# Attention softmax in an encoder kernel: sum with the bias and maximum in one operation by quarters, probabilities normalised on ScalarE

## The chip, the core and the metric

The kernel runs on one core of a Trainium2 chip. The core's engines run beside each other, each with a queue of its own that is worked off in order: TensorE (PE; its weight loads are listed as PEld), VectorE (DVE), ScalarE (ACT), GpSimd (POOL) and SyncE (SP, which issues DMAs). They meet through semaphores. The metric is the device time of one execution in microseconds; lower is better.

## The reference

An encoder of 2 layers over x of 512 positions by 1024 channels in float32. A layer is

```
x += 1/2 * SwiGLU(RMSNorm(x))
x += W_o( g_na * NA(h) W_na + g_f * FNet(h) W_f ),   h = RMSNorm(x)
x += 1/2 * SwiGLU(RMSNorm(x))
```

and a final RMSNorm ends it. NA is neighbourhood attention on the grid of 8 rows by 64 columns, with 8 heads of 64 channels. The columns go in 4 blocks of 16 queries; a block sees a band of 32 key columns, so a query has 8 x 32 = 256 keys, of which those outside its window of 16 columns are masked:

```
s = einsum(q, k) * 64 ** -0.5 + bias        # bias: learned, relative, per head
s = where(col_ok, s, -inf)
p = softmax(s, axis=-1)                     # over 256 keys
o = einsum(p, v)
```

FNet is the real part of a 2-D Fourier transform per channel group. The change is inside the softmax.

## The kernel before

All matmuls are made in float32 precision from two rounded parts: a helper `split` (L286 to L292) has ACT write the rounded high part and DVE the difference, and `mm3` (L281 to L284) issues three matmuls, high by high, high by low, low by high. Weights come by DMA in granules of 128 x 1024 (L150, on SP; some are added to another by a DMA of POOL at L152) and are split in this way two granules ahead of their use; L288 and L289 are the two lines of it, and L291 and L292 the same with a scale. The SwiGLU stages and the gates use Strassen's products.

`stage_mixer` goes, per layer: norm, projections for the Fourier part and for v, the Fourier part, then attention, then the gates (in an order written out by hand for DVE and ACT) and the output.

Attention works on two heads at a time (`hp` of 0 to 3) and on two of the four query blocks at a time (`pr`), so it has 8 steps. One step i of the pipeline `att_step` issues three things: `att_out(i-2)` (probabilities by v, and the split of the result `o`), `att_trans(i-1)` (transposes of the probabilities on PE at L1003, two PSUM banks, each split into `p` by L288 and L289) and `att_scores(i)`. Behind each of steps 0 to 4 stands a projection of a next q or k (24 matmuls; `proj_T` multiplies by the norm's row R at L826 and splits); between the later ones stand rows of the Fourier output product (`fill`, whose results ACT copies out at L1058).

`att_scores` computes for both heads e the scores of 128 queries against 256 keys, for two blocks jj side by side: one PSUM bank of 128 x 512 per head, L972. A quarter below is one head and one block, 128 x 256. Then, before the change:

- DVE adds the bias tile (bias and mask together) to each bank and writes the 128 x 512 tile `s` in SBUF (L980), and takes the negated maximum of each quarter (L981, one instruction per head).
- ACT takes the exponential of each quarter with the negated maximum as its per-partition bias and sums it on the way (L987).
- DVE takes the reciprocal of the two sums of a head (L990) and multiplies the head's two quarters by them (L992).

The bias tiles `bm` are built by POOL (L955), which waits until DVE's L980 of two head pairs earlier has read the tile that it overwrites.

The program is written in one order. A planner then lays the instructions out on the engines before the run: by their place in the program, by when its own costs say that their inputs are due, and by free tiles; it fixes each engine's order. Only inside `tc.manual_schedule` does an engine keep the written order; attention is not inside one.

Of the kernel before, what the change touches and what calls it, by code (L numbers as in the profile page):

```python
# [13 lines left out]
AF = mybir.ActivationFunctionType  # L14
ALU = mybir.AluOpType
AX = mybir.AxisListType

P = 128
# [10 lines left out]
NEG = -1.0e30  # L29
# [63 lines left out]
def encoder_kernel(  # L93
# [3 lines left out]
    V, S, G, PE = nc.vector, nc.scalar, nc.gpsimd, nc.tensor  # L97
# [11 lines left out]
    def nm(s):  # L109
        uid[0] += 1  # L110
        return f"{s}_{uid[0]}"
# [8 lines left out]
    def bank(s="ps"):  # L120
        return pp.tile([P, T], F32, tag="ps", name=nm(s))
# [663 lines left out]
    def stage_mixer(l, norm, nxt):  # L785
        mp = mix_pool[0]

        def tmp(dt=F32, s="x"):
            return mp.tile([P, T], dt, tag="tmp", name=nm(s), bufs=8)
# [142 lines left out]
        o, q, k, bms = [], {}, {}, {}  # L932
# [28 lines left out]
        def att_scores(i):  # L961
            hp, pr = divmod(i, 2)
            (qh, ql), (kh, kl) = q[hp], k[hp]
            ps = [bank(), bank()]
            for jj in range(2):
                j = 2 * pr + jj
                ks = slice(BAND[j] * 64, BAND[j] * 64 + 256)
                qs = slice(j * P, (j + 1) * P)
                for i, (a, b) in enumerate(((qh, kh), (qh, kl), (ql, kh))):
                    for e in range(2):  # L970
                        r = slice(64 * e, 64 * e + 64)
                        PE.matmul(  # L972
                            ps[e][:, jj * 256 : (jj + 1) * 256], a[r, qs], b[r, ks], start=i == 0, stop=i == 2
                        )
            s_ = [tmp(s="s"), tmp(s="s")]
            nmx = sp.tile([P, 4], F32, tag="nmx", name=nm("nmx"), bufs=4)
            sm = sp.tile([P, 4], F32, tag="sm", name=nm("sm"), bufs=4)
            rs = sp.tile([P, 4], F32, tag="rs", name=nm("rs"), bufs=4)
            for e in range(2):
                V.tensor_tensor(s_[e], ps[e], bms[hp][e][:, pr : pr + 2, :].rearrange("p a b -> p (a b)"), ALU.add)  # L980
                V.tensor_reduce(  # L981
                    nmx[:, 2 * e : 2 * e + 2], s_[e].rearrange("p (a k) -> p a k", a=2), AX.X, ALU.max, negate=True
                )
            for e in range(2):
                for jj in range(2):
                    c, z = slice(jj * 256, (jj + 1) * 256), 2 * e + jj
                    S.activation(  # L987
                        s_[e][:, c], s_[e][:, c], AF.Exp, bias=nmx[:, z : z + 1], accum_out=sm[:, z : z + 1]
                    )
                V.reciprocal(rs[:, 2 * e : 2 * e + 2], sm[:, 2 * e : 2 * e + 2])  # L990
                se = s_[e].rearrange("p (a k) -> p a k", a=2)
                V.tensor_tensor(  # L992
                    se, se, rs[:, 2 * e : 2 * e + 2].unsqueeze(2).to_broadcast([P, 2, 256]), ALU.mult
                )
            return s_

        def att_trans(s_):
# [32 lines left out]
        def att_step(i):  # L1030
            if 0 <= i - 2 < 8:
                att_out(i - 2, pt_.pop(i - 2))
            if 0 <= i - 1 < 8:
                pt_[i - 1] = att_trans(sc.pop(i - 1))
            if i < 8:
                sc[i] = att_scores(i)
# [152 lines left out]
        bias = []  # L1189
# [281 lines left out]
```

## Time and profile before

| what | value |
|---|---|
| time, median of 3 runs | 1946.33 us (1942.85 to 1946.69) |
| time of the profiled execution | 1946.85 us |
| its span, first to last instruction | 1944.4 us |
| mean granted TensorE clock | 0.997 |
| attention of layer 1, of layer 2 | about 411 to 489 us, 1372 to 1450 us |
| exponentials, L987 | 64 of 128 x 256, mean 498 ns |

A row of a group reads: line, engine, operation, written tile <- read tiles, shapes, count, then busy time in us and mean ns of one, then the idle time of the engine just before them and what ended it. A row of a timeline reads: start in us from the span's start, length in us, engine, line, operation, tiles, count; the bracket is idle time before it and what ended that. The chain of waits is followed back from the last instruction: at each piece to what released it or to the instruction before it on its engine; a piece called issue is time in which the engine waited for nothing that the profile shows. The rows of the windows give a stretch and its length, then the busy time of each engine and its instructions, the clock, the DMA share and GB/s. All lines are of the code printed above.

### The profile page before, as it was taken

What the parts mean: (1) busy time and instruction counts of PE and PEld (TensorE: products, weight loads), DVE (VectorE), ACT (ScalarE), POOL (GpSimd) and SP (SyncE); (2) the same over time, 40 slices, a digit from 0 to 9 for tenths busy, and PEclk for the clock granted to TensorE, in tenths of its full rate; (3) what the DMA queues carried; (4) which work ended last, traced back from release to release, by engine and by line L of the source; (5) the groups of instructions that cost most, each with busy time, mean ns of one, the idle gap of its engine ahead of it and who ended that gap; (6) DMA issues with size and microseconds to landing.
All of it is one profiled execution on the core that took longest, in us unless ns stands there. A gap on an engine that the chain in (4) does not pass through costs nothing.

```text
span 1944.4 us, 24590 instructions
## 1 busy us (share of the span) xinstructions
PE 1912.6 (98%) x8997; PEld 1583.5 (81%) x8997; DVE 1624.1 (84%) x1945; ACT 1127.3 (58%) x1605; POOL 213.1 (11%) x252
## 2 busy tenths in 40 slices
PE   9999999999999999999999999999999999999996
PEld 7788888888778888888888888888887888888885
DVE  8878899698788877889977878996878887877998
ACT  6655666455556655566655556663555566555654
POOL 0001010300111010001000000102101110100012
PEclk9999999999999999999999999999999999999998
DMA  8777498321997567749857665965039975766692
GB/s 284 199 201 194 148 255 306 105 60 56 261 231 190 139 187 204 181 153 263 240 142 207 177 169 176 289 219 147 28 116 243 235 198 132 196 181 162 186 286 97
DMA packets 105448, 361.82 MB, mean 186 GB/s; under 512 B 12016, under 2 KB 14192, under 8 KB 105328
## 3 DMA queue, kind: packets, MB, share of 16 engines
q1 hardware_dynamic: 76848, 264.01, 39.7%
q0 software_dynamic: 27328, 94.39, 26.3%
q10 hardware_dynamic: 1152, 1.86, 0.3%
q8 instruction: 70, 1.15, 0.2%
q14 instruction: 50, 0.41, 0.1%
HBM read 354.97 MB, written 2.10 MB: 184 GB/s over the span
## 4 chain that ended last, share of the span: by engine, by line
PE 78%; DVE 13%; DMA 3%; issue 3%; ACT 3%; ACTq 0%; SPq 0%; POOL 0%; DVEq 0%; POOLq 0%
PE A L282 8%; PE A L284 8%; PE A L283 8%; PE o L283 5%; PE o L284 5%; PE o L282 5%; PE B L283 4%; PE B L284 4%; PE B L282 4%; PE ps L282 4%; PE ps L283 4%; PE ps L284 4%; DVE wlo L289 4%; DMA raw<-in_wst_dram 3%; PE C L283 2%
## 5 line engine op out<-in xcount | busy, mean ns | idle before, releaser
L289 DVE TENSOR_TENSOR wlo<-raw,whi 128x1024 fp32r<-128x1024 f32 (+1 forms) x522 | 628.1, 1209 | 252.9 <-ACT whi L288 251.9
L288 ACT ACTIVATE whi<-raw 128x1024 fp32r<-128x1024 f32 (+1 forms) x522 | 540.1, 1037 | 496.6 <-PE A L284 126.3
L152 POOL DMA_DIRECT2D raw<-in_wst_dram x152 | 131.2, 878 | 1338.4 <-DMA raw<-in_wst_dram 814.4
L170 DVE TENSOR_TENSOR raw<-raw,raw 128x1024 f32<-128x1024 f32 (+1 forms) x128 | 150.9, 1189 | 2.4
L283 PE MATMUL A<-wlo,xh 128*128 128x512 f32 x384 | 150.0, 391 | 2.8 <-DVE wlo L173 2.2
L284 PE MATMUL A<-whi,xl 128*128 128x512 f32 x384 | 149.6, 389 | 0.0
L282 PE MATMUL A<-whi,xh 128*128 128x512 f32 x384 | 149.4, 390 | 0.0
L172 ACT ACTIVATE whi<-raw 128x1024 fp32r<-128x1024 f32 x76 | 78.9, 1038 | 68.3 <-PE B L284 33.2
L173 DVE SCALAR_TENSOR_TENSOR wlo<-raw,whi 128x1024 fp32r<-128x1024 f32 x76 | 89.8, 1193 | 13.4 <-ACT whi L172 13.4
L283 PEld LDWEIGHTS A<-wlo,xh 128*128 128x128 f32 x384 | 72.1, 188 | 19.8 <-DVE wlo L173 4.0
L282 PEld LDWEIGHTS A<-whi,xh 128*128 128x128 f32 x384 | 71.9, 188 | 15.7 <-ACT whi L172 0.8
L284 PEld LDWEIGHTS A<-whi,xl 128*128 128x128 f32 x384 | 72.1, 188 | 14.9
L466 ACT ACTIVATE sn<-A 128x512 f32<-128x512 f32 x96 | 56.8, 598 | 41.8 <-PE A L284 41.7
L282 PE MATMUL A<-whi,t3h 128*128 128x512 f32 x192 | 75.1, 391 | 2.4 <-ACT sn L466 2.4
L282 PE MATMUL B<-whi,t1h 128*128 128x512 f32 x192 | 76.1, 398 | 0.4 <-ACT whi L288 0.4
L283 PE MATMUL A<-wlo,t2h 128*128 128x512 f32 x192 | 74.8, 390 | 0.5 <-DVE wlo L289 0.5
L283 PE MATMUL C<-wlo,xh 128*128 128x512 f32 x192 | 74.8, 390 | 0.5 <-DVE wlo L289 0.5
L283 PE MATMUL B<-wlo,t1h 128*128 128x512 f32 x192 | 75.0, 391 | 0.2
L282 PE MATMUL C<-whi,xh 128*128 128x512 f32 x192 | 74.8, 391 | 0.2 <-ACT whi L288 0.2
L282 PE MATMUL A<-whi,t2h 128*128 128x512 f32 x192 | 74.9, 392 | 0.0
L283 PE MATMUL A<-wlo,t3h 128*128 128x512 f32 x192 | 74.9, 390 | 0.0
L284 PE MATMUL B<-whi,t1l 128*128 128x512 f32 x192 | 74.9, 390 | 0.0
(352 smaller groups left out, 4944.1 us busy)
## 6 DMA issues: line engine op xcount, KB each, us to landing
raw<-in_wst_dram SPq DMA_DIRECT2D x463, 512.0 KB
raw<-in_wst_dram POOLq DMA_DIRECT2D x168, 512.0 KB, 7.8
raw<-in_wst_dram SPq DMA_DIRECT2D x30, 256.0 KB
vs<-v SPq DMA_DIRECT2D x12, 256.0 KB
bw<-in_rpb_dram SPq DMA_DIRECT2D x32, 68.0 KB
x<-in_xin_dram SPq DMA_DIRECT2D x4, 512.0 KB
raw<-in_wst_dram POOLq DMA_DIRECT2D x8, 256.0 KB, 8.4
dft<-in_dft_dram POOLq DMA_DIRECT2D x8, 256.0 KB, 5.4
```

The costliest lines, as they stand in the source:

```text
L152: G.dma_start(out=self.t, in_=wst[GRAN_AT[self.plus]][:, 0 : self.n], accum_op=ALU.add)
L170: V.tensor_tensor(t, t, self.add.t, ALU.add)
L172: S.activation(hi, t, AF.Copy, scale=-1.0)
L173: V.scalar_tensor_tensor(lo, t, -1.0, hi.bitcast(F32), ALU.mult, ALU.subtract)
L282: PE.matmul(ps, lh, rh, start=start, stop=False, skip_group_check=again)
L283: PE.matmul(ps, lh, rl, start=False, stop=False, skip_group_check=again)
L284: PE.matmul(ps, ll, rh, start=False, stop=stop, skip_group_check=again)
L288: S.activation(hi, src, AF.Copy)
L289: V.tensor_tensor(lo, src, hi.bitcast(F32), ALU.subtract)
L466: S.activation(t[:, b, :], ps[b], AF.Copy)
```

## The change

The sum with the bias is made by quarters, with an operation that also gives the quarter's minimum: it writes s = -(scores + bias) and, beside it, the minimum of s, started from 1e30. That minimum is the negated maximum of the sum. The exponentials undo the sign with a scale of -1. After the exponentials and reciprocals of both heads, ACT multiplies each quarter by its reciprocal as a copy with a per-partition scale; DVE's multiplication goes. So one step has on DVE 4 such sums and 2 reciprocals in place of 2 sums, 2 maxima, 2 reciprocals and 2 products, and on ACT 4 exponentials and 4 copies in place of 4 exponentials.

```diff
             for e in range(2):
-                V.tensor_tensor(s_[e], ps[e], bms[hp][e][:, pr : pr + 2, :].rearrange("p a b -> p (a b)"), ALU.add)
-                V.tensor_reduce(
-                    nmx[:, 2 * e : 2 * e + 2], s_[e].rearrange("p (a k) -> p a k", a=2), AX.X, ALU.max, negate=True
-                )
+                for jj in range(2):
+                    c, z = slice(jj * 256, (jj + 1) * 256), 2 * e + jj
+                    V.tensor_tensor_reduce(
+                        s_[e][:, c], ps[e][:, c], bms[hp][e][:, pr + jj, :], -1.0, -NEG, ALU.add, ALU.min, nmx[:, z : z + 1]
+                    )
             for e in range(2):
                 for jj in range(2):
                     c, z = slice(jj * 256, (jj + 1) * 256), 2 * e + jj
                     S.activation(
-                        s_[e][:, c], s_[e][:, c], AF.Exp, bias=nmx[:, z : z + 1], accum_out=sm[:, z : z + 1]
+                        s_[e][:, c], s_[e][:, c], AF.Exp, scale=-1.0, bias=nmx[:, z : z + 1], accum_out=sm[:, z : z + 1]
                     )
                 V.reciprocal(rs[:, 2 * e : 2 * e + 2], sm[:, 2 * e : 2 * e + 2])
-                se = s_[e].rearrange("p (a k) -> p a k", a=2)
-                V.tensor_tensor(
-                    se, se, rs[:, 2 * e : 2 * e + 2].unsqueeze(2).to_broadcast([P, 2, 256]), ALU.mult
-                )
+            for e in range(2):
+                for jj in range(2):
+                    c, z = slice(jj * 256, (jj + 1) * 256), 2 * e + jj
+                    S.activation(s_[e][:, c], s_[e][:, c], AF.Copy, scale=rs[:, z : z + 1])
             return s_
```

## The prediction

> **What bounds the kernel now.** I read the page's busy line first, then the attention stretch by windows of 9 us (one attention step each), then the chain of waits in it, then the matmul starts in the timeline.
>
> ```profile
> PE 1912.6 (98%) x8997; PEld 1583.5 (81%) x8997; DVE 1624.1 (84%) x1945; ACT 1127.3 (58%) x1605; POOL 213.1 (11%) x252
> ```
>
> TensorE (PE) is never long without work, so an edit on other engines can win only where PE visibly waits for them. The windows (span length, then PE, PEld, DVE, ACT, POOL busy) show where that is in layer 1's attention:
>
> ```profile
> 412.00:421.00 9.00, 8.38 (x47) 6.37 (x46) 8.30 (x15) 4.83 (x13) 0.00 (x0) 1.00 0.00 1
> ...
> 439.00:448.00 9.00, 8.30 (x52) 7.00 (x52) 8.30 (x15) 5.07 (x14) 4.55 (x6) 1.00 0.10 25
> ...
> 457.00:466.00 9.00, 9.00 (x62) 7.71 (x60) 7.23 (x15) 5.20 (x15) 0.00 (x0) 1.00 0.19 58
> ```
>
> VectorE (DVE) is busy 8.30 of 9 us and ScalarE (ACT) about 5: DVE is the tight neighbour, and PE loses 0.6 to 0.7 us in each of two windows. The chain of waits agrees. From 413.8 to 453 us it runs through DVE and ACT; one step of it:
>
> ```profile
> 440.82 1.19 DVE s L980 x2
> 442.01 0.61 DVE nmx L981
> 442.62 0.02 issue
> 442.64 0.62 ACT s L987 x3
> ...
> 443.97 0.87 DVE s L992
> 444.84 0.60 DVE q L826
> 445.44 0.08 DVE rs L990
> ```
>
> Scores come out at L980; ACT may start the exponentials only after both adds and a maximum (1.8 us); the products at L992 end at 446.6. The matmul rows tell who paid:
>
> ```profile
> 445.60 0.49 PE L1003 MATMUL ps<-ident,s 128*128 128x128 f32 x3
> 446.79 0.74 PE L1003 MATMUL ps<-ident,s 128*128 128x128 f32 x5 [0.70 <-DVE s L992]
> ```
>
> Transposes start 0.11 us apart, so the fourth was due at 445.93 and lost 0.87. A matmul's row (0.39) is longer than its pitch (0.23), so busy time hides part of each loss; I count start to start. Counted so, transposes come late in layer 1 by 0.67 (at 417.86), 0.27, 0.20, 0.08, 0.87 and 0.18: **2.27 us**. Layer 2 gives 0.67, 0.27, 0.20, 0, 0.88, 0.18: 2.21 us. Together 4.5 us is all that a faster softmax can return directly. They belong to steps 0 (two), 1, 2, 3 and 4; in steps 5 to 7 the transposes are not late.
>
> **The change, part by part.** It touches 8 steps in each of 2 layers. The rows (busy, then mean ns):
>
> ```profile
> L992 DVE TENSOR_TENSOR s<-s,rs 128x512 f32<-128x512 f32 x16 | 12.2, 762 | 0.5
> ...
> L980 DVE TENSOR_TENSOR s<-ps,bm 128x512 f32<-128x512 f32 x16 | 10.2, 681 | 0.0
> L981 DVE TENSOR_REDUCE nmx<-s 128x2 f32<-128x512 f32 x16 | 10.2, 676 | 0.0
> ...
> L990 DVE RECIPROCAL rs<-sm 128x2 f32<-128x2 f32 x16 | 2.6, 162 | 4.9 <-ACT s L987 4.6
> ...
> L921 DVE TENSOR_TENSOR fy<-ps,fq 128x256 f32<-128x256 f32 x4 | 1.7, 420 | 0.2
> ```
>
> Removed from DVE per step: 2 adds, 2 maxima, 2 products, 2 x (0.681 + 0.676 + 0.762) = 4.24 us. The products vary: 0.69 alone, up to 1.10 while POOL builds bias tiles.
>
> Added on DVE: 4 sums with minimum over 128x256. No row shows this operation. Below, it costs what L921 does (same shape, one operand in PSUM): 0.42, less the 0.08 by which neighbours overlap (two L980 rows of 0.68 span 1.28), so 0.34. Above, it makes two passes plus a small write, 0.42 + 0.42 + 0.16 - 0.16 = 0.84. I take one pass plus a small 128x2 operation like L990, less the overlap: 0.42 + 0.16 - 0.08 = 0.50, nearest to L921 because the shape and operands are its own. That is 2.0 us per step (1.4 to 3.4), so **DVE is relieved by 4.24 - 2.0 = 2.2 us per step** (0.9 to 2.8). The Trainium skill (VectorE: DVE Perf Modes, section on two Vector instructions with no wait between them) says that an operation which also writes its accumulator is two instructions, which speaks for a price above 0.34; no DVE row here shows the second one.
>
> Added on ACT: 4 copies over 128x256 with a per-partition scale. The exponentials have that shape and a per-partition bias, row 0.498, and start 0.49 apart with a read-out of the sum between them. A copy has no read-out (its part of the pitch is 0.09): 0.40 to 0.49, I take 0.41, as a plain overlapped row. That is 1.6 us per step; ACT goes from 5.2 to 6.9 of 9 us. The exponentials' scale of -1 and the new start value are immediates on rows already paid for. The Trainium skill (ScalarE: Activation LUTs, rules for kernel authors) says to put a multiplication on VectorE, not ScalarE. Here 0.76 on DVE becomes 2 x 0.41 = 0.82 on ACT, so by price alone the rule holds narrowly; what it would give is the third rival.
>
> What decides is the latency from the scores to the transposes. For the step that starts on DVE at 440.73:
>
> - before: exponentials 442.64 to 444.63, products done 444.8 and 446.6.
> - after: sums end 441.23, 441.73, 442.23, 442.73; exponentials start 441.28 (the first needs only its own quarter), 441.8, 442.3, 442.8 and end at 443.3; the first reciprocal runs behind the sums at 442.8, the second at 443.6, after the last read-out; copies 443.3 to 444.2 and 444.2 to 445.0.
>
> The transposes were due at 445.60, so there are 0.6 us to spare where 0.87 was lost. Steps 1 to 7 should not wait. Step 0 starts at 413.81 because DVE is behind with the Fourier rows before it: last sum 415.8, copies of the first head done at 417.2 and of the second at 418.0, transposes due at 417.19. PE keeps about 0.3 us of its 0.95.
>
> What is late next: PE itself, which then paces attention. POOL and SP: the bias tiles and the weight loads that wait for DVE L980 (SP issues at 460.80 and 477.82) wait for the fourth sum instead, 2.0 after a step's start where 1.28 stood. The weight loaded at 477.82 is next split by ACT at 486.62 without a wait, so 0.7 us is covered; without cover it would cost that 0.7 once a layer. No DMA is added or moved. Behind each copy on ACT stand the weight split (1.04), the q split (0.62) and the evictions of o and p; the exponentials ended 1.3 us earlier, so the 1.6 of copies put these back 0.3 us, and weights are split two granules ahead.
>
> After attention, PE hands over at 489 us to a stretch in a fixed order (DVE and weight loads to 550). Its first work follows PE's last matmul (ACT's split at 488.95 is released by PE), so an earlier end shifts it whole.
>
> **Sum.** 2.27 + 2.21 - 2 x 0.3 = 3.9 us, from the profiled execution: 1946.85 (span 1944.4 and 2.4 around it) - 3.9 = 1942.95. That execution is 0.5 above the median 1946.33, so the median should be **1942.4**. 0.2% is 3.9 us, about what a measurement of this kernel can tell from no change; the forecast lies on it.
>
> **Rivals.**
>
> *Nothing is won.* The new operation is two passes (0.84): sums end 3.4 us after the start, the last exponential at 444.7, copies at 446.3. That is close to the old 446.6, and DVE is relieved by 0.9 only. Or the gain is used up by weight loads that don't move. Time 1946.3. For it: no row shows the operation. Against it: L921 shows two streams, one from PSUM, read in one pass.
>
> *More is won.* From 503 to 550 PE loses about 4 us per layer start to start, mostly behind DVE, and 2.2 us less DVE work per step may let the planner lay later work closer. Half of that in both layers is 4 us more: 1938.5. Against it: DVE's order there is written by hand.
>
> *Slower: ACT's queue becomes the late one.* The mechanism is order, not price. Engine orders are fixed beforehand by the planner's own clock; if it lays the weight split and the q split (1.04 + 0.62 = 1.66) between exponentials and copies, the copies end at 446.7 where transposes are due at 445.6: 1.1 late. It decides once more than the spare 0.6 is laid there. In all 8 steps of both layers that is 16 x 1.1 = 17, less the 4.5 that was lost anyway, +13: 1959. In half the steps +4 to +5: 1951. For it: ACT runs exactly these two after the exponentials now (444.63 and 445.57). Against it: the copies stand earlier in the program, and the first pair's sums are ready before the last exponential ends. By the Trainium skill's rule above (ScalarE: Activation LUTs) the multiplication is on the wrong engine, and this is the form that it would take.
>
> **How the numbers follow.** Forecast 0.62 (1941 to 1944; 0.42 of it beyond 0.2%, as the planner may close small gaps too, 0.20 within); more 0.05; nothing 0.13; slower 0.20. Faster 0.42 + 0.05 = 0.47, same 0.20 + 0.13 = 0.33, slower 0.20. The range goes from 1938.5 to 1951, where the slower case's half and the dear operation are in.
>
> **What would show it.** Right: sums near 0.5 us pitch, first exponential 0.55 us after the first sum starts (1.9 now), DVE near 6 of 9 us in windows of the first five steps, ACT near 7, PE 9.00 in all of them but the first, no wait of PE L1003 but in step 0. Wrong: a pitch over 0.8, PE L1003 waiting for ACT's copies in several steps, a split of weights between exponentials and copies, or the same PE loss shown later, at weight loads after 503 us.

## The result and the profile after

| what | before | after |
|---|---|---|
| time, median of 9 runs each | 1946.33 us (1942.49 to 1949.6) | 1938.61 us (1936.37 to 1942.41) |
| ratio, 95% interval | 1 | 0.9968 (0.996 to 0.9976) |
| profiled execution, its span | 1946.85, 1944.4 us | 1937.62, 1935.8 us |
| PE late at transposes, layer 1 and 2 | 2.47 and 2.41 us | 0.23 and 0.22 us |
| last transpose of layer 1 starts at | 483.07 us | 480.60 us |

The fourth line is counted from matmul start to matmul start in the trace, as in the prediction, but with every loss over 0.02 us in it, which is why before has 4.9 and not 4.5.

The changed kernel is faster, by 7.7 us between the medians where 3.9 was forecast. First the busy line and the same three windows of attention as before (columns as before: PE, PEld, DVE, ACT, POOL, clock, DMA share, GB/s):

```profile
PE 1908.2 (99%) x8997; PEld 1581.6 (82%) x8997; DVE 1582.0 (82%) x1977; ACT 1150.5 (59%) x1669; POOL 217.8 (11%) x252
```

```profile
412.00:421.00 9.00, 8.99 (x51) 7.19 (x50) 6.30 (x17) 6.36 (x17) 0.00 (x0) 1.00 0.00 1
439.00:448.00 9.00, 9.00 (x58) 7.67 (x57) 6.29 (x18) 6.88 (x18) 4.08 (x6) 1.00 0.16 58
457.00:466.00 9.00, 9.00 (x58) 7.69 (x57) 5.09 (x19) 6.48 (x18) 0.00 (x0) 1.00 0.17 58
```

PE is full in the two windows that had 8.38 and 8.30. DVE fell from 8.30 to 6.3 of 9 us, ACT rose from 5 to 6.9. The groups of attention in layer 1 give the durations that no row of before had:

```profile
L988 ACT ACTIVATE s<-s,nmx 128x256 f32<-128x256 f32 x32 | 15.9, 499 | 13.5 <-DVE nmx L982 13.5
...
L995 ACT ACTIVATE s<-s,rs 128x256 f32<-128x256 f32 x32 | 13.6, 496 | 0.0
...
L982 DVE CUSTOM_DVE_ANT_0 s<-ps,bm 128x256 f32<-128x256 f32 x32 | 11.6, 419 | 0.0
...
L982 DVE DVE_READ_ACCUMULATOR2_ANT nmx<- 128x1 f32 x32 | 2.7, 83 | 0.0
```

The new sum takes 419 ns, as a plain sum of that shape does (L921, 420), and the read-out of its minimum is a second instruction of 83 ns. What one step looks like, on DVE, then ACT, then PE:

```profile
439.85 0.41 DVE L982 CUSTOM_DVE_ANT_0 s<-ps,bm 128x256 f32<-128x256 f32 x1
440.18 0.08 DVE L982 DVE_READ_ACCUMULATOR2_ANT nmx<- 128x1 f32 x1
440.18 0.42 DVE L982 CUSTOM_DVE_ANT_0 s<-ps,bm 128x256 f32<-128x256 f32 x1
...
440.53 0.42 DVE L982 CUSTOM_DVE_ANT_0 s<-ps,bm 128x256 f32<-128x256 f32 x1
```

```profile
440.30 0.51 ACT L988 ACTIVATE s<-s,nmx 128x256 f32<-128x256 f32 x1 [1.74 <-DVE nmx L982]
...
441.80 0.49 ACT L988 ACTIVATE s<-s,nmx 128x256 f32<-128x256 f32 x1
...
442.29 1.69 ACT L995 ACTIVATE s<-s,rs 128x256 f32<-128x256 f32 x4
```

```profile
444.18 1.04 PE L1004 MATMUL ps<-ident,s 128*128 128x128 f32 x8
445.14 0.97 PE L972 MATMUL ps<-q,q 64*128 64x256 f32 x12
```

The read-out starts where the next sum starts, so it costs DVE nothing: the pitch is 0.35 us. The first exponential starts 0.45 us after the first sum (439.85 to 440.30). Before, it took 1.91 (440.73 to 442.64); the chain of waits, which shows the sums from 440.82 on, leaves out the first 0.09 us of them. Their row in the timeline of before is:

```profile
440.73 1.28 DVE L980 TENSOR_TENSOR s<-ps,bm 128x512 f32<-128x512 f32 x2
```

The eight transposes run as one group, and the next work, L972, follows them without a gap. The last copy ends at 443.98 and the first transpose starts at 444.18: 0.2 us are left over. The waits in attention of layer 1 (waiting row, releaser: us in all, times, longest) say the same:

```profile
ACT s L988 <- DVE nmx L982: 13.5, 8, 2.0
...
PEld ps L1004 <- ACT s L995: 0.2, 1, 0.2
```

Before, ACT waited 21.8 us for the maxima, and PE waited at the transposes for both DVE's products and ACT. One weight load of 0.2 us is what is left, in step 0.

### The profile page after: what moved, and what is told of

Same layout as the page of the kernel before. It is cut to its first block, busy times and chain, and to the rows that moved or that the text cites. A ratio compares the mean times of both kernels' runs of the same rounds, so it can differ in the third digit from the quotient of the medians.

```text
span 1935.8 us, 24624 instructions
## 1 busy us (share of the span) xinstructions
PE 1908.2 (99%) x8997; PEld 1581.6 (82%) x8997; DVE 1582.0 (82%) x1977; ACT 1150.5 (59%) x1669; POOL 217.8 (11%) x252
## 3 DMA queue, kind: packets, MB, share of 16 engines
q8 instruction: 70, 1.15, 0.2%
## 4 chain that ended last, share of the span: by engine, by line
PE 84%; DVE 9%; DMA 2%; issue 2%; ACT 2%; SPq 0%; ACTq 0%; POOL 0%; DVEq 0%; POOLq 0%
PE A L282 8%; PE A L284 8%; PE A L283 8%; PE o L283 5%; PE o L284 5%; PE ps L282 5%; PE o L282 5%; PE ps L283 5%; PE ps L284 5%; PE B L283 4%; PE B L284 4%; PE B L282 4%; DVE wlo L289 3%; DMA raw<-in_wst_dram 2%; PE C L283 2%
## 5 line engine op out<-in xcount | busy, mean ns | idle before, releaser
L289 DVE TENSOR_TENSOR wlo<-raw,whi 128x1024 fp32r<-128x1024 f32 (+1 forms) x522 | 623.6, 1201 | 270.4 <-ACT whi L288 269.8
L283 PE MATMUL B<-wlo,xh 128*128 128x512 f32 x192 | 74.8, 390 | 0.4 <-DVE wlo L289 0.4
```

Of the source, the lines that this page charges most:

```text
L283: PE.matmul(ps, lh, rl, start=False, stop=False, skip_group_check=again)
L289: V.tensor_tensor(lo, src, hi.bitcast(F32), ALU.subtract)
```

## The experiments

**The theory**: PE waits for the probabilities because the way from scores to transposes is too long, and the early first exponential, which needs only its own quarter, is what shortens it. **The rival**: DVE was overloaded (8.3 of 9 us), and any work taken off it, by either half of the change, gives time back.

### The two kernels again

Neither is edited; this shows what two executions of the same program differ by.

> The kernel before, unchanged, for a second profile and for what two rounds of one kernel differ by. Expected: ratio to before 1.000 within 0.002. The waits at the transposes L1003 come back to within 0.1 us of the first profile (2.3 us in layer 1, 2.2 in layer 2), since they repeat from layer to layer. If the losses outside attention are chance, those at the gates (3.7 and 3.2 us in the first profile) and near the end (7 us at 1920 us) come out otherwise here; if they belong to the kernel, they come back.

> The changed kernel, unchanged, for a second profile. Expected by the theory that the gain is the waits at the transposes: PE's shift across the attention of each layer comes back at 2.5 us (5 us in both), and the other 3.6 us of the first pair of profiles (8.6 in the spans) change from profile to profile; ratio to before about 0.997. By the rival that the change also helps the gates and the end: the end's loss is again some 6 us less than in the kernel before.

Measured: 0.9998 (0.9989 to 1.0007) and 0.9975 (0.9966 to 0.9984), medians 1945.73 and 1941.36 beside 1946.86. Late at transposes: 2.46 and 2.35 us in before, 0.22 and 0.22 in after, the same as the first time to 0.06. The spans differ by 1944.9 - 1939.5 = 5.4, where the first pair differed by 8.6. One wait near the end shows why (waits of PE in the last 140 us; first before, then after, then after again):

```profile
PE o L283 <- DVE wlo L289: 5.3, 1, 5.3
```

```profile
PE o L283 <- DVE wlo L289: 1.0, 1, 1.0
```

```profile
PE o L283 <- DVE wlo L289: 4.2, 1, 4.2
```

The same program waits 1.0 us in one execution and 4.2 in the next; before waits 5.3 and 4.5. So this wait, which was 4.3 us of the first difference, isn't the change's.

### Only the sum

The product stays on DVE, behind the fused sum by quarters.

```diff
-            for e in range(2):
-                for jj in range(2):
-                    c, z = slice(jj * 256, (jj + 1) * 256), 2 * e + jj
-                    S.activation(s_[e][:, c], s_[e][:, c], AF.Copy, scale=rs[:, z : z + 1])
+                se = s_[e].rearrange("p (a k) -> p a k", a=2)
+                V.tensor_tensor(
+                    se, se, rs[:, 2 * e : 2 * e + 2].unsqueeze(2).to_broadcast([P, 2, 256]), ALU.mult
+                )
```

> The fused sum with minimum, with the multiplication left on DVE. Theory (latency from the scores to the transposes decides, and the early first exponential carries it): exponentials start 0.5 us after the first sum instead of 1.9, products of both heads are done 3.3 to 4.5 us after it, transposes due 4.4 after it; nearly all waits at the transposes go, ratio about 0.997 to 0.998, the same as the whole change. Rival (DVE's load decides): DVE gets only 1.2 of the 2.7 us per step that the whole change takes from it, so about half of the gain, ratio 0.9985.

Measured: 0.9968 (0.9956 to 0.9979), 1940.34 us, six runs. All of the gain is there without the copies, and the rival's 0.9985 lies outside the interval. The windows of this kernel:

```profile
412.00:421.00 9.00, 9.00 (x52) 7.35 (x51) 8.35 (x19) 5.31 (x14) 0.00 (x0) 1.00 0.00 1
439.00:448.00 9.00, 9.00 (x58) 7.71 (x57) 8.38 (x20) 5.57 (x14) 5.98 (x6) 1.00 0.12 40
```

This is the reading that decides against the rival: in these two windows DVE is as busy as it was before (8.35 and 8.38 beside 8.30), and PE is late by 0.00 us in both layers. Over the whole execution DVE is relieved a little, to 1611.6 us from 1624.1, which is 0.8 us for each of the 16 steps; the whole change takes 2.6 a step off it (1582.0) and wins no more. In the timeline the products of this step run from 440.71 and 441.88 and end at 442.90, and the transposes start at 444.32: 1.4 us to spare, where the whole change has 0.2.

### Only the product moved to ACT

Sum and maximum are those of before, the copies on ACT stay.

```diff
-                for jj in range(2):
-                    c, z = slice(jj * 256, (jj + 1) * 256), 2 * e + jj
-                    V.tensor_tensor_reduce(
-                        s_[e][:, c], ps[e][:, c], bms[hp][e][:, pr + jj, :], -1.0, -NEG, ALU.add, ALU.min, nmx[:, z : z + 1]
-                    )
+                V.tensor_tensor(s_[e], ps[e], bms[hp][e][:, pr : pr + 2, :].rearrange("p a b -> p (a b)"), ALU.add)
+                V.tensor_reduce(
+                    nmx[:, 2 * e : 2 * e + 2], s_[e].rearrange("p (a k) -> p a k", a=2), AX.X, ALU.max, negate=True
+                )
```

> The multiplication on ACT, with sum and maximum as before. Theory (latency): exponentials start 1.9 us after the first sum and end at 3.9, copies at 4.7 and 5.5 where the transposes are due at 4.4, so 0.5 to 0.7 us late in each of 16 steps, 8 to 11 us, against the 4.5 us of before: ratio 1.002 to 1.003, slower than before. Rival (DVE's load): DVE is relieved by 1.5 us per step, so about half of the gain, ratio 0.9985.

Measured: 1.0018 (1.0009 to 1.0027), 1949.88 us: slower. Its first window and PE's transposes of step 0:

```profile
412.00:421.00 9.00, 8.13 (x44) 5.86 (x42) 6.20 (x12) 5.42 (x17) 0.00 (x0) 1.00 0.00 1
```

```profile
418.21 0.84 PE L1003 MATMUL ps<-ident,s 128*128 128x128 f32 x4 [0.87 <-ACT s L994]
418.98 0.39 PE L972 MATMUL ps<-q,q 64*128 64x256 f32 x2
```

DVE is relieved (6.20 of 9) and PE has more holes than before (8.13 beside 8.38): late by 3.81 and 3.85 us. Scores (L972) stand between the transposes on PE. The reason is in ACT's row of one step:

```profile
443.61 0.51 ACT L987 ACTIVATE s<-s,nmx 128x256 f32<-128x256 f32 x1 [3.19 <-DVE nmx L981]
...
445.60 1.69 ACT L994 ACTIVATE s<-s,rs 128x256 f32<-128x256 f32 x4
```

All four copies stand behind all four exponentials. Sums begin at 441.71, so the first head is ready 4.8 us after them (446.5); before, DVE multiplied the first head while ACT was at the second head's exponentials, and it was ready after 4.1 (440.73 to 444.84).

The theory's sign is right and the sum of its lateness near (7.7 us where 8 to 11 were expected), but not its spread: it expected every step to be late, and in each layer three of the eight are, steps 0, 3 and 6, with 1.8, 0.8 and 1.15 us of layer 1's 3.8. In step 6 the order of ACT's queue may have a part in it too: a weight split (1.04 us from 471.80) stands between the third and the fourth exponential, and a copy-out of the Fourier rows between the copies.

By the Trainium skill's rule (ScalarE: Activation LUTs, rules for kernel authors) a multiplication belongs on VectorE; before and this kernel agree, with 1.0018 for the copies. Behind the fused sum the time doesn't tell the two forms apart (0.9968 with the product on DVE, 0.9968 and 0.9975 with the copies). What the trace adds is a reason that isn't the price: four copies take 1.69 us, two products 1.4 to 2.2, but the products run beside the exponentials and the copies don't.

### Quarters without the fused operation

Sum and maximum become two plain operations by quarters. First with the copies on ACT, then with the product on DVE, where the second has also the edit of the product shown above.

```diff
-                    V.tensor_tensor_reduce(
-                        s_[e][:, c], ps[e][:, c], bms[hp][e][:, pr + jj, :], -1.0, -NEG, ALU.add, ALU.min, nmx[:, z : z + 1]
-                    )
+                    V.tensor_tensor(s_[e][:, c], ps[e][:, c], bms[hp][e][:, pr + jj, :], ALU.add)
+                    V.tensor_reduce(nmx[:, z : z + 1], s_[e][:, c], AX.X, ALU.max, negate=True)
...
-                        s_[e][:, c], s_[e][:, c], AF.Exp, scale=-1.0, bias=nmx[:, z : z + 1], accum_out=sm[:, z : z + 1]
+                        s_[e][:, c], s_[e][:, c], AF.Exp, bias=nmx[:, z : z + 1], accum_out=sm[:, z : z + 1]
```

> Sum and maximum by quarters as two plain operations each, the multiplication on ACT: the changed kernel without the fused operation. Theory (latency from the scores to the transposes): the planner lays two sums and two maxima per head, so the first exponential starts 1.0 us after the first sum, the last ends at 3.5, copies end at 4.3 and 5.1 where the second head's transposes are due at 4.6: 0.3 to 0.5 late in 16 steps, 5 to 8 us, against the 4.5 of before: ratio 1.000 to 1.002. Rival (DVE's load decides): DVE is relieved by 1.4 us per step, about half of the gain, ratio 0.9985.

> The kernel before, with sum and maximum by quarters as plain operations, multiplication on DVE: not less work on DVE (4 x 0.34 x 2 = 2.7 us per step where 2.5 stood) but an earlier first exponential. Theory (latency): first exponential at 1.0 us after the first sum instead of 1.9, products at 3.6 and 4.6 to 5.9 instead of 4.1 and 5.9, against transposes due at 4.4: a part of the waits goes, ratio 0.998 to 0.9995. Rival (DVE's load decides): DVE carries 0.2 us per step more, ratio 1.000 to 1.002.

Measured: 0.9999 (0.999 to 1.0007) with the copies and 0.9981 (0.9973 to 0.999) with the product on DVE, medians 1943.96 and 1941.04 beside 1944.72. The first is where the theory put it (1.000 to 1.002), with 4.4 us late, a little under its 5 to 8, and the rival's 0.9985 lies outside the interval. The second is the sharper test: it takes no work off the engine that the rival calls overloaded. DVE's busy time over the execution is 1624.2 us beside 1624.1, in 64 more instructions. One of its windows, and DVE's and ACT's start of the step in it:

```profile
439.00:448.00 9.00, 9.00 (x59) 7.68 (x57) 8.83 (x19) 5.30 (x14) 6.08 (x6) 1.00 0.00 0
```

```profile
440.96 0.75 DVE L982 TENSOR_TENSOR s<-ps,bm 128x256 f32<-128x256 f32 x2
```

```profile
442.07 0.51 ACT L987 ACTIVATE s<-s,nmx 128x256 f32<-128x256 f32 x1 [2.39 <-DVE nmx L983]
```

DVE is busy 8.83 of 9 us, more than before's 8.30, and PE is full; the first exponential starts 1.1 us after the first sum (1.91 before, 0.45 after). Late at transposes: 1.10 and 1.17 us, less than half of before. By the rival nothing could be won here (1.000 to 1.002), and 0.9981 was measured.

### The copies twice, and no normalisation at all

Two tests of ACT's part. One adds a plain copy in place behind each copy:

```diff
                     S.activation(s_[e][:, c], s_[e][:, c], AF.Copy, scale=rs[:, z : z + 1])
+                    S.activation(s_[e][:, c], s_[e][:, c], AF.Copy)
```

> The changed kernel, with a second plain copy of each quarter in place behind each normalising copy: 1.6 us more on ACT between exponentials and transposes, 8.5 of 9 us busy. It is the prediction's slower rival, made on purpose. Theory (latency): the copies end at 5.7 us after the first sum instead of 4.1, where the last transposes are due at 5.3 or earlier; 0.6 to 1.2 us late in 16 steps, 10 to 19 us, less the gain of 5: ratio 1.002 to 1.007. Rival (ACT has room as long as it is not full): ratio 0.997 as the change.

The other takes the copies out, so that probabilities stay unnormalised:

```diff
-            for e in range(2):
-                for jj in range(2):
-                    c, z = slice(jj * 256, (jj + 1) * 256), 2 * e + jj
-                    S.activation(s_[e][:, c], s_[e][:, c], AF.Copy, scale=rs[:, z : z + 1])
```

> The changed kernel without the four copies: it leaves the normalisation of the probabilities out. Theory (PE alone paces attention now): nothing is left to win, ratio 0.997, within 0.001 of the change, waits at the transposes 0 to 0.2 us per layer. Rival (the copies on ACT still hold something back, in attention or at the gates): another 2 to 4 us, ratio 0.995.

Measured: 0.9997 (0.9988 to 1.0006) with the copies twice, 0.9977 (0.9968 to 0.9986) without them. The second is as both the theory and the trace of the change have it: PE is late by 0.00 us, and the time can't be told from the change's own (0.9975). The copies on ACT are covered but for step 0, and next to nothing is left to win there.

The first missed on both sides. The theory asked for 1.002 to 1.007, the rival for 0.997; the gain just went. ACT and then DVE of one step show where the theory's size failed:

```profile
442.64 0.91 ACT L995 ACTIVATE s<-s,rs 128x256 f32<-128x256 f32 x2 [0.27 <-DVE rs L991]
443.46 0.71 ACT L996 ACTIVATE s<-s 128x256 f32<-128x256 f32 x2
444.07 0.89 ACT L995 ACTIVATE s<-s,rs 128x256 f32<-128x256 f32 x2
444.87 0.71 ACT L996 ACTIVATE s<-s 128x256 f32<-128x256 f32 x2
```

```profile
441.20 1.33 DVE L289 TENSOR_TENSOR wlo<-raw,whi 128x1024 fp32r<-128x1024 f32 x1
```

A plain copy takes 0.31 us of ACT's time and not 0.40 (two run in 0.71, with the overlap at their ends), so a step got 1.2 us more and not 1.6. And the planner laid the engines out anew: the weight split's part on DVE (wlo), which stood ahead of the next step's sums, now runs behind them, and in this step the sums start 3.66 us after the transposes of the step before (436.17 to 439.83) where the change has 4.59. That took back 0.9 of the 1.2. PE is late by 2.2 us in each layer, which is not far from before's 2.47 and 2.41, but at other places:

```profile
457.00:466.00 9.00, 8.74 (x56) 7.29 (x55) 4.88 (x16) 8.48 (x23) 0.00 (x0) 1.00 0.16 58
466.00:475.00 9.00, 8.73 (x56) 7.32 (x55) 4.24 (x14) 7.58 (x22) 0.00 (x0) 1.00 0.01 2
```

PE now loses 0.5 us in each of steps 5 and 6, which had no wait before, and DVE is idle half of the time. In these two steps of both layers, and in no other, work stands behind the exponentials and ahead of the last copies, a copy-out of the Fourier rows in step 5 and a weight split in step 6:

```profile
460.56 0.60 ACT L1060 ACTIVATE fs<-ps 128x512 f32<-128x512 f32 x1
...
470.89 1.04 ACT L288 ACTIVATE whi<-raw 128x1024 fp32r<-128x1024 f32 x1
```

This fits the mechanism of the prediction's slower rival, work laid between exponentials and copies, with 0.5 us a step and not 1.1; no run takes this work away again, so its share isn't shown apart. The direction is the theory's (a longer way costs, with DVE at 4 to 5 of 9), the size isn't.

### The six forms side by side

PE's lateness at transposes, both layers together in us, and the ratio to before:

| sum and maximum | product on DVE | copies on ACT |
|---|---|---|
| by halves, two operations | 4.9; 1 (before) | 7.7; 1.0018 (1.0009 to 1.0027) |
| by quarters, two operations | 2.3; 0.9981 (0.9973 to 0.999) | 4.4; 0.9999 (0.999 to 1.0007) |
| by quarters, fused | 0.0; 0.9968 (0.9956 to 0.9979) | 0.45; 0.9968 (0.996 to 0.9976), again 0.9975 (0.9966 to 0.9984) |

Down each column the way to the first exponential gets shorter and the lateness falls; in each row the copies on ACT add lateness: 2.8, 2.1 and 0.45 us. The lateness against before's 4.9 gives the ratio by itself: +2.8 us is +0.14% (measured +0.18), -2.6 is -0.13% (-0.19), -0.5 is -0.03% (-0.01), -4.9 is -0.25% (-0.32), -4.4 is -0.23% (-0.32 and -0.25). Every one of these lies within the interval measured, but for the first run of the change, whose surplus is taken up below.

The length of attention itself, from its first score to its last transpose, closes the gap. In layer 1 it is 72.40 us before and 72.29 in before again, 69.87 and 69.86 in the change and its second profile, and layer 2 repeats each to 0.05. Both layers together, and as a ratio to 1946.33 us:

| kernel | attention shorter by, us | ratio from it | ratio measured |
|---|---|---|---|
| the change, both profiles | 5.0 | 0.9974 | 0.9968 and 0.9975 |
| only the sum | 5.9 | 0.9970 | 0.9968 |
| no normalisation | 5.4 | 0.9972 | 0.9977 |
| quarters, product on DVE | 2.8 | 0.9985 | 0.9981 |
| copies twice | 1.2 | 0.9994 | 0.9997 |
| quarters, copies on ACT | 0.7 | 0.9996 | 0.9999 |
| only the copies | -3.6 | 1.0018 | 1.0018 |

All of these lie within the intervals, the change's first run too. In this stretch the change is still 0.4 us a layer longer than the sum alone (69.87 beside 69.46) and 0.2 longer than without the copies (69.67), too little for the times to show.

## Why the prediction was right, and where it was off

**What bounds the kernel: right.** PE paces attention, and its waits at the transposes were nearly all that was to be had: 4.9 us by the table's count, and the kernel without any such wait is at 0.9968 as well. What came on top lies in the scores, see the sum below.

**The mechanism: right, with its halves confused.** The forecast let the latency from scores to transposes decide, and the early first exponential does carry it. But it put the relief of DVE (2.2 us per step) in bold, and DVE's load is not the cause: 8.4 of 9 us with the product on DVE gives no wait, 6.2 with the copies on ACT gives more waits than before. It also costed both halves as one change. One half wins all of it, and the other loses by itself; the fused sum hides what the copies cost.

**The new operation: mis-sized.** Taken at 0.50 us, bounded by 0.34 and 0.84; it has a pitch of 0.35, at the lower bound. The Trainium skill (VectorE: DVE Perf Modes, section on two Vector instructions with no wait between them) was right that an operation with an accumulator is two instructions: the second row is there, at 83 ns. But it starts with the next sum and takes no time of its own, so it does not speak for a price above 0.34. So the relief of DVE was too small in the forecast as well: over the execution its busy time fell by 42.1 us (1624.1 to 1582.0), 2.6 for each of 16 steps where 2.2 was forecast.

**The copies: right.** Forecast 0.41 us each, ACT near 7 of 9. The four take 1.69 us, 0.40 apart, and ACT is at 6.9. In all eight steps of layer 1 ACT's copies (L995) follow its exponentials (L988) with no other work between; that the weight split stood there was the slower rival's condition, and in the changed kernel it did not occur.

**The spare time: mis-sized.** Forecast 0.6 us; 0.2 was measured in the same step (443.98 to 444.18). With the sums at 0.35 the copies end 4.13 us after the first sum, earlier than the 4.3 forecast. But PE, which no longer waits, comes to the transposes 1.42 us sooner than before (445.60 to 444.18), and DVE's first sum only 0.88 (440.73 to 439.85); the forecast held both still. By this count the slower rival was nearer than its 0.6 said. But the count is strict, since the first transposes don't read the last copy: with the copies twice, the transposes start at 445.05, 0.5 us before the last copy ends (444.87 + 0.71), and only 0.11 us is lost in that step.

**Step 0: mis-sized.** The forecast left 0.3 us of PE's loss there in each layer; 0.2 is left.

**The sum: too small by 1.1 us.** Forecast 3.9 us. From the first score to the last transpose the change gave 2.5 us in each layer, the same in both pairs of profiles: 5.0. Of the 1.1 us more than forecast, 0.4 are losses at transposes too small for the forecast's count (4.9 beside 4.5), and 0.15 are step 0's. The rest is in the scores. Before, the transposes of steps 0 and 1 are cut in two by scores, so scores stand in 10 groups a layer, and in 8 after; the first score behind a transpose starts 0.20 us after it. From start to start the 96 scores of a layer take 7.71 us before and 7.31 to 7.32 after, 0.8 us in both layers; 0.2 is lost again at other matmuls. The forecast had this only as a remark in its chances, that small gaps may close too.

**The rest of the first measurement is not the change.** 8.6 us between the first two spans less 5.0 leaves 3.6. The wait near the end differs by 4.3 there and by 0.3 in the second pair. The stretch of 75 us after each attention, where the rival with more gained looked for it, lost 4.57 and 3.95 us in before and 5.45 and 4.75 in before again, 3.43 and 4.83 in after and 4.49 and 6.09 in after again: it varies by more between executions of one kernel than between the two kernels. So the rival with more gained (half of the 4 us per layer after 503 us) is not shown, though the first time, 1938.61, lies on its number. That time is below the forecast's 1941 to 1944 and only 0.1 us inside its range; 5.0 us alone would give 1941.3, and the second measurement gave 1941.36. The 2.7 us below that are luck and not the mechanism, as far as the traces show. What makes the wait near the end long or short stays open.

**The other rivals.** *Nothing is won*: its condition, two passes at 0.84, is refuted by the 419 ns row; its time came with quarters in two operations and copies on ACT (0.9999), where the sum and maximum of one quarter do take two passes, 0.66 us. The gain was not used up by weight loads either: near 967 us, PE is 3.9 and 2.6 us ahead of the first profile of before in the two profiles of the change. *Slower by ACT's queue*: not in the changed kernel, but the mechanism is real, as the copies alone (1.0018) and the copies twice (all of the gain gone) show. The queue's length costs time by itself: steps 0 and 3 of the copies alone, with nothing laid between, have 2.6 of the 3.8 us. The rival's own form, work laid between exponentials and copies, stands in step 6 of the copies alone (1.15 us) and in steps 5 and 6 of the copies twice (1.0 of 2.2).

## What to carry to other kernels

Where an engine that is full waits for a chain of others, measure the chain's length, not its members' load: cut the piece that the next engine starts on so that it starts early, and keep work that could run beside the next link off that link's own queue. Test the halves of a change apart, since one may pay for the other: here the fused sum alone gives what the change gives, with 1.4 us to spare and not 0.2. And run both kernels twice before explaining the whole of a difference of 0.4%: here a wait elsewhere came and went with 3 to 4 us, where the change is worth 5. The length of the stretch that was changed, from one matmul to another, repeated to about 0.1 us and told more than the whole time.

## What the runs showed of the hardware that was not expected

- DVE's read-out of an accumulator (83 ns) starts before the operation that fills it has ended by its row (0.41 from 439.85, read-out at 440.18), together with the next sum: four sums with minima take 4 x 0.35 us.
- A copy on ACT with a per-partition scale has a pitch of 0.40 us for 128 x 256, one without a scale 0.31.
- DVE's product, which reads SBUF alone, takes 0.69 us by itself and up to 1.10 while POOL builds bias tiles. POOL's own rows average 720 ns with the copies on ACT and 1032 with the products on DVE behind the fused sum: there they run from 0.71 us beside fused sums to 1.16 to 1.18 beside products, and to 1.71 beside the DVE part of the splits of a weight and of q (L289, L292). The fused sum, with one operand in PSUM, takes 415 to 422 ns beside POOL in both.
